# Steps moved by a slot in a hybrid decoder block's branches, and 96 instead of 128 stationary columns in one product of an inverse's doubling

## The chip, the cores and the metric

The kernel runs on one core of one Trainium2 chip. The metric is the device time of one execution in microseconds. The core has five engines with instruction queues of their own: PE (TensorE, matmuls, with weight loads shown apart as PEld), DVE (VectorE), ACT (ScalarE), POOL (GpSimd) and SP (SyncE, which here only issues DMAs). Each executes its instructions in order, and waits on semaphores for the others.

## The reference

One layer of a decoder on x of 256 x 2048, in float32. `h` is a normalised x; one input projection of h feeds three branches, whose outputs are gated, projected and summed; an MLP follows.

```python
h = rmsnorm(x, g_pre_mix)
proj = h @ w_in
aq, ak, av, az, ab, aa, bq, bf, bi, bz, cq, gates = split(proj)
qkv = silu(causal_dwconv(concat([aq, ak, av]), conv_a))
oa = gated_deltanet(aq, ak, av, sigmoid(ab), logdecay)   # 8 heads of 128, chunks of 64
oa = gated_head_norm(oa, az, gn_a)
ob = gated_head_norm(hgrn2(bq, bf, bi, lb), bz, gn_b)    # 8 heads of 128, chunks of 64
oc = memory_attention(cq, rmsnorm(mem, g_mem), w_kv_mem)
ga, gb, gc = split(sigmoid(gates))
merged = ga * (oa @ w_br_a) + gb * (ob @ w_br_b) + gc * (oc @ w_br_c)
x = x + rmsnorm(merged @ w_out, g_post_mix)
h2 = rmsnorm(x, g_pre_mlp)
x = x + rmsnorm(square(relu(h2 @ w_mlp_in)) @ w_mlp_out, g_post_mlp)
```

In `gated_deltanet` each chunk solves a unit lower triangular system of 64 x 64; in `hgrn2` the forget gate is `lb + (1 - lb) * sigmoid(f)`, taken in logarithms; `gated_head_norm` divides each head's output by its root mean square and multiplies by `silu(z)`.

## The kernel before

**Weights.** All large products are a stream of weight tiles of 256 rows by 512 columns (512 KB, 128 partitions by 2 x 512). SP's queue loads each into one of four buffers `w`. ACT casts it to float32r (`wh`), DVE forms the rest (`wl = w - wh`), and PE multiplies the two halves of the activations with them in three products: h with `wh`, h with `wl`, l with `wh` (`load_w`, `split_w`, `unit`). `wh` and `wl` have four buffers each as well. A tile of `unit` is 12 matmuls of 128 x 512; `unit_joined` forms a transposed result, with 16 matmuls of 512 and 256 columns per pair of halves. Counted from 0 in program order, tiles 192 to 199 belong to the forget projection of head group 1 (BF), 200 to 207 to its query (BQ), 208 to 223 to its BI and BZ, and 224 to 271 to branch 0: four turns j, each with eight tiles of the gate projection (G) and four of `w_br`. Branch 1 begins with tile 272 and its first `w_br` tile is 280; tiles from 320 on are `w_out`.

**Background steps.** Between the tiles, generators do the small work: `gen_a` (the delta rule of one head group), `gen_b` (the HGRN2 recurrence of one head group), `head_out` (the head norm, the transposes `oT` on PE, and their split into `oh` and `ol`), `gen_merge`, and the steps of `conv`, `z_evac` and `forget`, which go ahead of the others (`ahead_of_all`). `tick` runs after each tile and takes as many steps as a rate says, R1 to R4 by the part of the program. What a step issues stands at that place in the program; each `yield` ends a step. `pin` and `issue_after` keep an instruction at its place in its engine's queue; the other instructions of a step are put in order by the scheduler, by its own times and priorities. `drain` runs all steps that are left at once.

**Logarithms.** `exp_ln_table` issues an Abs on ACT and then the load of ACT's table for exponential and logarithm; Exp and Ln follow. It is used by `forget` (buffer `fe`) and by `gen_b` (buffer `bd`). Sigmoid and SiLU use another table.

**The inverse.** `gen_a` forms the inverse of the triangular system by doubling. At s = 32 blocks of 32 become blocks of 64: a product `pw`, a copy to `W`, and a second product `pzt`, whose stationary side is W of 128 x 128 for each of 8 blocks (two matrices of 64 in each), whose moving side is half of the columns of XT, and whose result is copied under a mask into XT. It runs once for each head group.

**Branches.** `branch(gi, o, w_br)` takes the gate's unit, a sigmoid of its PSUM into `sg`, the unit of `o` with `w_br`, and adds the product to `mg`. `o` is filled by `head_out`. Before branch 0 a loop pumps until `oa[1]` is there; behind it `drain` finishes `gen_b`, so that `ob` is there for branch 1. `load_gbc` issues two DMAs of 512 KB on ACT's queue; they broadcast a gain row.

Of the kernel before, what the change touches and what calls it, by code (L numbers as in the profile page):

```python
# [17 lines left out]
P = 128  # L18
# [15 lines left out]
KG = 2  # L34
BL = 16
WB = 4
R1, R2, R3, R4 = 1.1, 1.2, 1.2, 1.2


@with_exitstack  # L40
def tile_trunk(ctx: ExitStack, tc, a):
# [47 lines left out]
    def g4(name, shape=(P, 1024), dt=F32):  # L89
        return gp.tile(list(shape), dt, tag="g", name=nm(name))  # L90
# [11 lines left out]
    def bank(name):  # L102
        return pbp.tile([P, 512], F32, tag="bp", name=nm(name))
# [60 lines left out]
    def drain():  # L164
        while bg:
            pump(1)
# [608 lines left out]
    def head_out(o, z, rq, dst, hg):  # L775

        sq = g4("sq", (P, 8, P))
        A.activation(sq, o, AF.Square)
        ss = small("ss", 8)
        V.tensor_reduce(out=ss, in_=sq, axis=AX.X, op=ALU.add)  # L780
        yield
        if rq is not None:
            V.tensor_tensor(out=ss, in0=ss, in1=rq, op=ALU.mult)
            V.tensor_tensor(out=ss, in0=ss, in1=rq, op=ALU.mult)
        sc = rstd_of(ss, 8, P)
        if rq is not None:
            sc2 = small("sc2", 8)
            V.tensor_tensor(out=sc2, in0=sc, in1=rq, op=ALU.mult)
            sc = sc2
        on = g4("on", (P, 8, P))  # L790
        for b in range(8):
            V.scalar_tensor_tensor(out=on[:, b, :], in0=o[:, b, :], scalar=sc[:, b:b + 1], in1=z[:, b, :],
                                   op0=ALU.mult, op1=ALU.mult)
            if b % 4 == 3:
                yield
        hi, lo = g4("oh", (P, 4, S), F32R), g4("ol", (P, 4, S), F32R)
        for hh in range(2):
            pt = bank("oT")
            for q in range(2):
                for t in range(NT):  # L800
                    T.transpose(pt[:, q * S + t * P:q * S + (t + 1) * P], on[:, t * 4 + hh * 2 + q, :], ident)
            split_psum(pt.rearrange("p (q s) -> p q s", q=2), hi[:, hh * 2:hh * 2 + 2, :], lo[:, hh * 2:hh * 2 + 2, :])
        yield
        dst[hg] = (hi, lo)

    def gen_a(hg, kc, qc, vc, z):
# [167 lines left out]
        for s in (s_ for s_ in (2, 4, 8, 16, 32, 64) if s_ >= 2 * BL):  # L974
            last = s == 64
            pw = bank("pw")
            if last:

                for b in range(8):
                    T.matmul(pw[64:128, b * 64:(b + 1) * 64], U[0:64, b, 64:128], X[0:64, b, 0:64], start=True, stop=True)  # L980
                A.copy(W[64:128, :, 0:64], pw[64:128, :].rearrange("p (b s) -> p b s", b=8))
                yield
                pzt = bank("pzt")
                for b in range(8):
                    T.matmul(pzt[0:64, b * 64:(b + 1) * 64], W[64:128, b, 0:64], XT[64:128, b, 64:128],
                             start=True, stop=True)
                A.copy(XT[0:64, :, 64:128], pzt[0:64, :].rearrange("p (b s) -> p b s", b=8))
                yield
                break
            for b in range(8):  # L990
                T.matmul(pw[:, b * 64:(b + 1) * 64], U[:, b, :], half_view(X, s, False)[:, b], start=True, stop=True)
            A.copy(half_view(W, s, False), pw.rearrange("p (b n s) -> p b n s", b=8, s=s))
            yield
            pzt = bank("pzt")
            for b in range(8):
                T.matmul(pzt[:, b * 64:(b + 1) * 64], W[:, b, :], half_view(XT, s, True)[:, b],
                         start=True, stop=True)
            V.copy_predicated(half_view(XT, s, True), half_mask(mT[s], s, True),
                              pzt.rearrange("p (b n s) -> p b n s", b=8, s=s))
            yield  # L1000
            if s == 32:

                pt = bank("X")
                for b in range(8):
                    T.transpose(pt[0:64, b * 64:(b + 1) * 64], XT[0:64, b, 0:64], ident[0:64, 0:64])
                A.copy(X[0:64, :, 0:64], pt[0:64, :].rearrange("p (b i) -> p b i", b=8))
                yield
                continue
            for t in range(NT):
                pt = bank("X")  # L1010
                for h in range(4):
                    T.transpose(pt[:, h * P:(h + 1) * P], XT[:, t * 4 + h, :], ident)
                A.copy(X[:, t * 4:t * 4 + 4, :], pt.rearrange("p (h i) -> p h i", h=4))
            yield
# [67 lines left out]
    def branch(gi, o, w_br):  # L1082
        oact = act_of(o)
        for j in range(4):
            ps = unit(hact, KT, w_in, OFF_G + gi * D + 512 * j)
            sg = g4("sg", (P, NT, 512))
            own_table(A.activation(sg, ps.rearrange("p (t n) -> p t n", t=NT), AF.Sigmoid))
            ps = unit(oact, 8, w_br, 512 * j).rearrange("p (t n) -> p t n", t=NT)
            if gi == 2:
                mg[j] = g4("mg", (P, NT, 512))  # L1090
                V.tensor_tensor(out=mg[j], in0=ps, in1=sg, op=ALU.mult)
            else:
                V.tensor_tensor(out=sg, in0=ps, in1=sg, op=ALU.mult)
                V.tensor_tensor(out=mg[j], in0=mg[j], in1=sg, op=ALU.add)
            if gi == 1:
                bg.append(gen_merge(j))
# [4 lines left out]
    def forget(ps, hg):  # L1101

        t, g = g4("ft", (P, 4, S)), g4("fg", (P, 4, S))

        def steps():
            e = g4("fe", (P, 4, S))
            exp_ln_table(e, ps)
            pin(A.activation(e, e, AF.Exp, scale=-1.0))
            pin(A.activation(e, e, AF.Ln, bias=1.0))
            yield  # L1110
            yield
            V.scalar_tensor_tensor(out=t, in0=ps, scalar=0.0, in1=e, op0=ALU.max, op1=ALU.add)
            yield
            for h in range(4):
                c = hg * 4 + h
                A.activation(t[:, h, :], t[:, h, :], AF.Exp, scale=-1.0, bias=lbl1[:, c:c + 1])
            V.scalar_tensor_tensor(out=g, in0=ps, scalar=0.0, in1=e, op0=ALU.min, op1=ALU.subtract)
            yield

        ahead_of_all(steps())  # L1120
        return t, g

    def gen_b(hg, k, g, q, v, z):
# [9 lines left out]
                yield  # L1133
        exp_ln_table(d, d)
        pin(A.activation(d, d, AF.Exp, scale=-1.0))
        pin(A.activation(d, d, AF.Ln, bias=1.0))
        kq, kqh, kql = g4("kq"), g4("kqdh", dt=F32R), g4("kqdl", dt=F32R)
        V.tensor_tensor(out=kq, in0=k.rearrange("p h s -> p (h s)"), in1=q.rearrange("p h s -> p (h s)"), op=ALU.mult)
# [139 lines left out]
        bg.append(gen_b(hg, k, g, q, v, z))  # L1278
    rate[0] = R4

    while oa[1] is None:
        pump(1)
    branch(0, oa, a["w_br_a"][0])
    drain()


    def load_gbc(src):
# [4 lines left out]
            r.append(t)  # L1292
        return r

    gbc = load_gbc(a["g_post_mix"])
    branch(1, ob, a["w_br_b"][0])

    def gb(c):
        return gbc[c // 2][:, c % 2 * 512:c % 2 * 512 + 512]
# [210 lines left out]
```

## Time and profile before

| what | value |
|---|---|
| three runs | 1806.97, 1805.63, 1805.83 us; median 1805.83 |
| the profiled execution | 1805.44 us |
| its span, from first to last instruction | 1803.7 us |
| mean granted TensorE clock | 0.997 |
| ACT, DVE busy | 50%, 64% of the span |
| chain of work that ended last | PE 83% of the span, DVE 1%, ACT 1% |

The page lists for one execution the busy time of each engine, what ended the idle time of a group of instructions, and the chain followed back from the last instruction. In rows of the timeline the columns are start and duration in us, engine, line, operation, result and sources by their names, size and count, and in square brackets the idle time ahead with the engine and buffer that ended it. All rows have line 56, since a helper issues every instruction; so the names of the buffers tell them apart. `128*128` is the part of the array that a matmul uses. A matmul's row is longer than its share of the engine, since matmuls are pipelined: the distance from start to start counts.

### The profile page before, as it was taken

The numbers are of one execution on the slowest core, as the hardware profiler recorded it, in microseconds if no ns is written. First come the engines' busy times: TensorE is split into PE (matmuls) and PEld (weight loads), VectorE is DVE, ScalarE is ACT, GpSimd is POOL, SyncE is SP. The second block draws the span as 40 slices with busy tenths as digits, with TensorE's granted clock in tenths as the row PEclk, the third lists the DMA queues.
The fourth block names the chain that finished last, engine by engine and source line by source line (L and its number), as shares of the span: only waits on it lengthen the run. The fifth ranks groups of instructions, "written<-read, shape, count | busy, mean of one in ns | idle before, by whom it ended". The sixth has DMA issues, their size and how long they took to land.

```text
span 1803.7 us, 23759 instructions
## 1 busy us (share of the span) xinstructions
PE 1787.2 (99%) x9137; PEld 1522.9 (84%) x9137; DVE 1152.7 (64%) x1599; ACT 901.8 (50%) x1148; POOL 59.7 (3%) x100
## 2 busy tenths in 40 slices
PE   9999999999999999999999999999999999999998
PEld 7888888888888888888788888888888888888886
DVE  6865768684867577696555557555655565655556
ACT  6645566454554464555444445544444444444433
POOL 0000000400120000000000000000000000000000
PEclk9999999999999999999999999999999999999999
DMA  8665545875487455555666674666666666656563
GB/s 268 204 192 166 175 148 165 240 204 151 154 214 216 122 154 175 149 187 174 189 186 186 215 235 149 191 193 192 193 187 197 192 216 187 197 184 197 187 196 136
DMA packets 176226, 336.60 MB, mean 187 GB/s; under 512 B 13656, under 2 KB 15472, under 8 KB 175728
## 3 DMA queue, kind: packets, MB, share of 16 engines
q1 hardware_dynamic: 169280, 325.10, 58.7%
q0 software_dynamic: 2304, 5.44, 1.6%
q10 hardware_dynamic: 4528, 4.54, 0.9%
q8 instruction: 71, 1.16, 0.3%
q14 instruction: 43, 0.35, 0.1%
HBM read 332.75 MB, written 2.29 MB: 186 GB/s over the span
## 4 chain that ended last, share of the span: by engine, by line
PE 83%; DVE 1%; ACT 1%; issue 0%; POOL 0%; DVEq 0%; POOLq 0%
PE mm L56 78%; PE pa L56 1%; PE kk L56 0%; PE pzt L56 0%; PE pw L56 0%; PE bo L56 0%; PE o L56 0%; DVE on L56 0%; DVE wl L56 0%; POOL r L329 0%; PE tr L56 0%; ACT L56 0%; PE y L56 0%; PE mgT L56 0%; ACT bd L56 0%
## 5 line engine op out<-in xcount | busy, mean ns | idle before, releaser
L56 DVE TENSOR_TENSOR wl<-w,wh 128x1024 fp32r<-128x1024 f32 (+1 forms) x610 | 738.3, 1219 | 523.3 <-ACT wh L56 446.9
L56 ACT CAST wh<-w 128x1024 fp32r<-128x1024 f32 (+1 forms) x610 | 636.3, 1050 | 728.3 <-PE mm L56 632.0
L56 PE MATMUL mm<-wh,hh 128*128 128x512 f32 x1152 | 366.2, 392 | 0.0
L56 PEld LDWEIGHTS mm<-wh,hh 128*128 128x128 f32 x1152 | 216.2, 188 | 44.4
L56 PE MATMUL mm<-wl,hh 128*128 128x512 f32 x576 | 224.6, 390 | 0.0
L56 PE MATMUL mm<-h2h,wh 128*128 128x512 f32 x960 | 224.4, 390 | 0.0
L56 PEld LDWEIGHTS mm<-h2h,wh 128*128 128x128 f32 x960 | 178.3, 188 | 35.8
L56 PE MATMUL mm<-wh,mh 128*128 128x512 f32 x512 | 199.2, 389 | 0.0
L56 PE MATMUL mm<-wl,mh 128*128 128x512 f32 x512 | 199.2, 389 | 0.0
L56 PE MATMUL mm<-wh,ml 128*128 128x512 f32 x512 | 199.2, 389 | 0.0
L56 PE MATMUL mm<-hh,wh 128*128 128x512 f32 x768 | 185.9, 393 | 0.8 <-ACT z L56 0.8
L56 PEld LDWEIGHTS mm<-hh,wh 128*128 128x128 f32 x768 | 141.9, 189 | 29.0 <-ACT z L56 1.0
L56 PEld LDWEIGHTS mm<-wl,hh 128*128 128x128 f32 x576 | 108.2, 188 | 21.3
L56 PEld LDWEIGHTS mm<-h2h,wl 128*128 128x128 f32 x960 | 119.3, 192 | 2.3
L56 PE MATMUL mm<-h2h,wl 128*128 128x256 f32 x960 | 120.3, 283 | 0.0
L56 PEld LDWEIGHTS mm<-wh,mh 128*128 128x128 f32 x512 | 96.1, 188 | 20.0
L56 PEld LDWEIGHTS mm<-wl,mh 128*128 128x128 f32 x512 | 96.1, 188 | 19.9
L56 PEld LDWEIGHTS mm<-wh,ml 128*128 128x128 f32 x512 | 96.1, 188 | 19.9
L56 PE MATMUL mm<-hh,wl 128*128 128x256 f32 x768 | 103.8, 287 | 2.7 <-DVE wl L56 2.7
L56 PEld LDWEIGHTS mm<-hh,wl 128*128 128x128 f32 x768 | 100.4, 194 | 6.5 <-DVE wl L56 2.9
L56 PE MATMUL mm<-wh,oh 128*128 128x512 f32 x128 | 50.2, 392 | 0.0
L56 PE MATMUL mm<-wh,mgh 128*128 128x512 f32 x128 | 50.0, 390 | 0.0
(336 smaller groups left out, 1775.4 us busy)
## 6 DMA issues: line engine op xcount, KB each, us to landing
w<-in_w_in SPq DMA_DIRECT2D x240, 512.0 KB, 4.1
w<-in_w_mlp_in SPq DMA_DIRECT2D x128, 512.0 KB, 3.9
w<-in_w_mlp_out SPq DMA_DIRECT2D x128, 512.0 KB, 4.1
w<-in_w_out SPq DMA_DIRECT2D x32, 512.0 KB, 4.4
w<-in_w_kv_mem SPq DMA_DIRECT2D x30, 512.0 KB, 5.3
w<-in_w_br_c SPq DMA_DIRECT2D x16, 512.0 KB, 3.8
w<-in_w_br_a SPq DMA_DIRECT2D x16, 512.0 KB, 4.5
w<-in_w_br_b SPq DMA_DIRECT2D x16, 512.0 KB, 4.0
```

Source lines behind the costliest of these rows:

```text
L56: ins = op(*args, **kwargs)
```

## The change

Six edits of order and one of size:

- R4, the rate of steps from branch 0 on, is 1.25 instead of 1.2.
- `head_out` has one more `yield`, between the scaling `on` and the transposes `oT`.
- The second product of the doubling at s = 32 uses 96 of the 128 columns of W, and its result and the masked copy have 96 partitions. The lower 32 rows of a 128-row block hold nothing that the mask lets through.
- `branch` has the loop that pumps until `o[1]` is there between the gate's unit and the unit of `w_br`. The loop before branch 0 and the `drain` behind it are gone.
- `forget` begins with an empty step, and has a step's end between Exp and Ln, and one empty step less behind.
- `gen_b` has a step's end between Exp and Ln of `bd`.
- The two DMAs of `gbc` for the mixer are issued behind branch 1 instead of ahead of it.

```diff
-R1, R2, R3, R4 = 1.1, 1.2, 1.2, 1.2
+R1, R2, R3, R4 = 1.1, 1.2, 1.2, 1.25
...
             if b % 4 == 3:
                 yield
+        yield
         hi, lo = g4("oh", (P, 4, S), F32R), g4("ol", (P, 4, S), F32R)
...
-            pzt = bank("pzt")
+
+            pzt, m = bank("pzt"), P - s
             for b in range(8):
-                T.matmul(pzt[:, b * 64:(b + 1) * 64], W[:, b, :], half_view(XT, s, True)[:, b],
+                T.matmul(pzt[0:m, b * 64:(b + 1) * 64], W[:, b, 0:m], half_view(XT, s, True)[:, b],
                          start=True, stop=True)
-            V.copy_predicated(half_view(XT, s, True), half_mask(mT[s], s, True),
-                              pzt.rearrange("p (b n s) -> p b n s", b=8, s=s))
+            V.copy_predicated(half_view(XT[0:m], s, True), half_mask(mT[s], s, True)[0:m],
+                              pzt[0:m].rearrange("p (b n s) -> p b n s", b=8, s=s))
             yield
...
             own_table(A.activation(sg, ps.rearrange("p (t n) -> p t n", t=NT), AF.Sigmoid))
+            while o[1] is None:
+                pump(1)
             ps = unit(oact, 8, w_br, 512 * j).rearrange("p (t n) -> p t n", t=NT)
...
         def steps():
+            yield
             e = g4("fe", (P, 4, S))
             exp_ln_table(e, ps)
             pin(A.activation(e, e, AF.Exp, scale=-1.0))
+            yield
             pin(A.activation(e, e, AF.Ln, bias=1.0))
-            yield
             yield
             V.scalar_tensor_tensor(out=t, in0=ps, scalar=0.0, in1=e, op0=ALU.max, op1=ALU.add)
...
         exp_ln_table(d, d)
         pin(A.activation(d, d, AF.Exp, scale=-1.0))
+        yield
         pin(A.activation(d, d, AF.Ln, bias=1.0))
...
-    while oa[1] is None:
-        pump(1)
     branch(0, oa, a["w_br_a"][0])
-    drain()
...
+    branch(1, ob, a["w_br_b"][0])
     gbc = load_gbc(a["g_post_mix"])
-    branch(1, ob, a["w_br_b"][0])
```

How the rows move is shown at three places. The numbers behind a name tell buffers of one name apart; each program has numbers of its own.

The first place is ACT's queue in the query projection of head group 1, where the gate `fe` of that group and the chain `bd` of gen_b(0) are taken. `wh_6042` is tile 202 of the program before:

```order
L56 CAST oh_5896<-oT_5898 128x512
L56 CAST oh_5896<-oT_5905 128x512
L56 COPY sum_5724<-mm_5725 128x512
L56 ACTIVATE bd_5941<-bd_5941 128x1024
L56 ACT_TABLE_LOAD
L56 ACTIVATE bd_5941<-bd_5941 128x1024
L56 COPY sum_5724<-mm_5755 128x512
L56 ACTIVATE bd_5941<-bd_5941 128x1024
L56 ACTIVATE fe_6018<-sum_5724 128x1024
L56 ACT_TABLE_LOAD
L56 ACTIVATE fe_6018<-fe_6018 128x1024
L56 CAST wh_6042<-w_6040 128x1024
```

In the changed program the same place reads so; `wh_6023`, `wh_6029`, `wh_6069` and `wh_6075` are tiles 202 to 205:

```order
L56 CAST wh_6023<-w_6021 128x1024
L56 CAST wh_6029<-w_6027 128x1024
L56 COPY sum_5700<-mm_5731 128x512
L56 CAST oh_5950<-oT_5952 128x512
L56 CAST oh_5950<-oT_5959 128x512
L56 ACTIVATE fe_6013<-sum_5700 128x1024
L56 ACT_TABLE_LOAD
L56 ACTIVATE fe_6013<-fe_6013 128x1024
L56 CAST wh_6069<-w_6067 128x1024
L56 ACTIVATE fe_6013<-fe_6013 128x1024
L56 CAST wh_6075<-w_6073 128x1024
```

The chain `bd` is no longer here (it begins behind tiles 206 and 207), and casts of weights stand ahead of `fe` and between its Exp and Ln.

The second place is DVE's queue at the head norm of gen_b(0), in branch 0, where `on` is what PE transposes. Before, with `wl_6977` tile 239:

```order
L56 TENSOR_REDUCE ss_6862<-sq_6860 128x8
L56 TENSOR_TENSOR sg_6777<-mm_6779,sg_6777 128x1024
L56 TENSOR_SCALAR v_6882<-ss_6862 128x8
L56 TENSOR_TENSOR wl_6977<-w_6974,wh_6976 128x1024
L56 SCALAR_TENSOR_TENSOR on_6886<-ob_6843,r_6884,z_5722 128x128 x4
L56 TENSOR_TENSOR mg_3790<-mg_3790,sg_6777 128x1024
L56 SCALAR_TENSOR_TENSOR on_6886<-ob_6843,r_6884,z_5722 128x128 x4
L56 TENSOR_TENSOR wl_7007<-w_7004,wh_7006 128x1024
```

And in the changed program, with `wl_6942` tile 239 and `wl_7025` tile 242:

```order
L56 TENSOR_TENSOR sg_6756<-mm_6758,sg_6756 128x1024
L56 TENSOR_TENSOR wl_6942<-w_6939,wh_6941 128x1024
L56 TENSOR_TENSOR mg_3790<-mg_3790,sg_6756 128x1024
L56 TENSOR_TENSOR wl_6969<-w_6966,wh_6968 128x1024
L56 TENSOR_TENSOR wl_6991<-w_6988,wh_6990 128x1024
L56 TENSOR_REDUCE ss_6937<-sq_6935 128x8
L56 TENSOR_SCALAR v_6957<-ss_6937 128x8
L56 SCALAR_TENSOR_TENSOR on_6961<-ob_6900,r_6959,z_5698 128x128 x8
L56 TENSOR_TENSOR wl_7025<-w_7022,wh_7024 128x1024
```

The merge (`sg`, `mg`) and three residuals now stand ahead of the head norm, whose rows follow each other. On PE the transposes of this head group stand behind the last matmul of tile 241 instead of tile 237, those of head group 1 behind tile 277 instead of in two parts round tiles 272 and 273.

The third place is ACT's queue in branch 0's second turn. Before, with `wh_7142` tile 246 and `wh_7172` tile 247:

```order
L56 CAST wh_7142<-w_7140 128x1024
L56 ACT_TABLE_LOAD
L56 ACTIVATE sg_7095<-mm_6893 128x1024
L56 ACT_TABLE_LOAD
L56 ACTIVATE qp_7092<-bm_6968 128x8x64
L56 CAST wh_7172<-w_7170 128x1024
```

And in the changed program, with `wh_7120` tile 246 and `wh_7141` tile 247:

```order
L56 CAST wh_7120<-w_7118 128x1024
L56 ACT_TABLE_LOAD
L56 ACTIVATE sg_7068<-mm_6854 128x1024
L56 ACTIVATE bd_7041<-bd_7041 128x1024
L56 ACT_TABLE_LOAD
L56 ACTIVATE bd_7041<-bd_7041 128x1024
L56 CAST kqdh_7094<-kq_7093 128x1024
L56 ACTIVATE bd_7041<-bd_7041 128x1024
L56 CAST wh_7141<-w_7139 128x1024
L56 CAST wh_7170<-w_7168 128x1024
```

The chain `bd` of gen_b(1) and the cast `kqdh`, which stood about four tiles earlier, are now in this gap between two casts of weights; `qp` has gone behind them.

## The prediction

> **What bounds the kernel now.** I read the page's first part, then PE's waits in the region that the diff touches, then the windows and timelines round each wait. Weight tiles are numbered from 0 in program order; that order is the same in both programs.
>
> ```profile
> PE 1787.2 (99%) x9137; PEld 1522.9 (84%) x9137; DVE 1152.7 (64%) x1599; ACT 901.8 (50%) x1148; POOL 59.7 (3%) x100
> ```
>
> PE is busy for 99% of the span. An edit can pay only by removing PE work, a PE wait, or time at a lowered clock. PE's waits between 600 and 900 us:
>
> ```profile
> PE mm L56 <- DVE wl L56: 2.7, 1, 2.7
> PE oT L56 <- DVE on L56: 2.1, 4, 1.1
> ```
>
> The first wait stands in PE's timeline, and the windows give the clock behind it (columns: stretch, length, busy time of PE, PEld, DVE, ACT and POOL, then granted clock, DMA share, GB/s):
>
> ```profile
> 638.96 3.97 PE L56 MATMUL mm<-hh,wl 128*128 128x256 f32 x16 [2.67 <-DVE wl L56]
> 639.00:645.30 6.30, 6.30 (x23) 5.62 (x24) 5.73 (x6) 4.15 (x7) 0.00 (x0) 0.51 0.62 168
> 645.30:680.00 34.70, 34.70 (x174) 29.76 (x173) 31.02 (x48) 21.85 (x25) 0.00 (x0) 1.00 0.61 182
> ```
>
> PE stood for 2.67 us, and in the 6.30 us that follow TensorE had 0.51 of its clock, which costs (1 - 0.51) x 6.30 = 3.09 us more. After 645.3 the clock is 1.00. One late tile thus costs 5.76 us. ACT's timeline says why it was late:
>
> ```profile
> 622.13 1.05 ACT L56 CAST wh<-w 128x1024 fp32r<-128x1024 f32 x1 [0.76 <-PE mm L56]
> ...
> 628.53 1.06 ACT L56 ACTIVATE bd<-bd 128x1024 f32<-128x1024 f32 x1 [0.28 <-DVE bd L56]
> ...
> 633.29 1.05 ACT L56 ACTIVATE fe<-sum 128x1024 f32<-128x1024 f32 x1
> 634.36 1.28 ACT L56 ACT_TABLE_LOAD   x1
> 635.65 1.06 ACT L56 ACTIVATE fe<-fe 128x1024 f32<-128x1024 f32 x1
> 636.62 1.03 ACT L56 CAST wh<-w 128x1024 fp32r<-128x1024 f32 x1
> ```
>
> And DVE's row behind it:
>
> ```profile
> 637.68 1.23 DVE L56 TENSOR_TENSOR wl<-w,wh 128x1024 fp32r<-128x1024 f32 x1 [4.51 <-ACT wh L56]
> ```
>
> From 628.53 to 636.62 ACT works without a gap on two logarithm chains (`bd` of gen_b(0), then `fe` of hg 1) and one PSUM copy, 8.09 us in which no weight is cast. Tile 202's cast is behind them; DVE had waited 4.51 us for it.
>
> **Tile 202: -2.67 and -3.09.** In the new order ACT casts tiles 202 and 203 ahead of the `fe` chain, tiles 204 and 205 one on each side of its last `fe`, and the `bd` chain comes two casts later still (first fence of the change). The longest run without a cast there is one sum copy, two `oh` casts, `fe`, the table load and `fe`: about 0.5 + 1.1 + 1.07 + 1.29 + 0.97 = 4.9 us by the starts above. Walking these rows against PE's pace, tile 204 is ready some 5.5 us before its first matmul. So the wait goes, and with it the stretch at half clock.
>
> By the Trainium skill ("TensorE: Matmul & The Clock Gate", the table of Part 1) the clock falls after at least one idle window of about 3.4 us. This trace shows 0.51 right behind 2.67 us, so here the measurement decides. By the page's figure alone the 3.09 would have another cause and would stay.
>
> **The oT waits: -1.14 and -0.98.** head_out transposes `on` on PE too early. Two rows of its waits:
>
> ```profile
> 755.35 1.12 PE L56 MATMUL oT<-ident,on 128*128 128x128 f32 x7 [1.14 <-DVE on L56]
> 869.04 0.55 PE L56 MATMUL oT<-ident,on 128*128 128x128 f32 x3 [0.35 <-DVE on L56]
> ```
> ```profile
> 740.00:760.00 20.00, 18.86 (x102) 15.79 (x101) 13.25 (x21) 9.37 (x12) 2.54 (x1) 1.00 0.46 135
> ```
>
> The first is hg 0's; the other three of the 2.1 us, 0.98 together, are hg 1's, in 863 to 869. The chain that `oT` needs, in ACT's and DVE's timelines:
>
> ```profile
> 745.96 0.59 ACT L56 COPY ob<-bo 128x512 f32<-128x512 f32 x1 [1.14 <-PE bo L56]
> 746.58 1.06 ACT L56 ACTIVATE sq<-ob 128x1024 f32<-128x1024 f32 x1
> ```
> ```profile
> 747.67 1.22 DVE L56 TENSOR_REDUCE ss<-sq 128x8 f32<-128x1024 f32 x1 [2.09 <-ACT sq L56]
> ...
> 749.94 0.16 DVE L56 TENSOR_SCALAR v<-ss 128x8 f32<-128x8 f32 x1
> ...
> 752.76 1.14 DVE L56 SCALAR_TENSOR_TENSOR on<-ob,r,z 128x128 f32<-128x128 f32 x4 [1.53 <-POOL r L329]
> ...
> 754.95 1.13 DVE L56 SCALAR_TENSOR_TENSOR on<-ob,r,z 128x128 f32<-128x128 f32 x4
> ```
>
> From the end of `bo` (745.9) the chain takes 10.2 us, because DVE does `sg` ahead of `v`, and `mg` between the two halves of `on`. In the new order these, and the residual that stood there, are out of it (second fence of the change). What is left is 747.67 - 745.96 + 1.22 = 2.93, `v` 0.16, POOL's power (749.94 + 0.16 to 752.76) 2.66, and twice 1.13 of `on`: 8.0 us. `oT` comes four weight tiles after `bo` instead of three. A tile is 12 slots, and a slot is (775.00 - 773.64) / 6 = 0.227 by the rows quoted further down, so that four are 10.9 us and the margin is 2.9 us. hg 1 has the same pattern. Both waits go; the 1.14 us one did not lower the clock (the window round it, below), so nothing more comes with it. For oa[1] the step is later in the same way, and no wait stood there.
>
> **The doubling's second product: -0.7.** Two groups of 8 matmuls (16 records), one per head group. The group of 128 columns, and the nearest rows of 64, with the matmuls round them:
>
> ```profile
> 424.12 1.89 PE L56 MATMUL pzt<-XT,W 128*128 128x64 f32 x16
> ...
> 426.14 0.39 PE L56 MATMUL mm<-wl,hh 128*128 128x512 f32 x1
> ```
> ```profile
> 431.95 0.39 PE L56 MATMUL mm<-wh,hh 128*128 128x512 f32 x1
> 432.27 1.14 PE L56 MATMUL pw<-X,U 64*64 64x64 f32 x16
> 433.34 0.50 PE L56 MATMUL mm<-wh,hh 128*128 128x512 f32 x1
> 433.68 0.39 PE L56 MATMUL mm<-wl,hh 128*128 128x512 f32 x1
> ```
>
> The 128-column group costs 426.14 - 424.12 less one slot, 1.79 us. The 64-column one costs 433.68 - 431.95 less two slots, 1.28 us, in which a matmul ahead of it holds 0.32 and one behind it 0.34 instead of 0.227: 0.21 us for going in and out, 1.07 for itself. No row has 96 columns. Halfway between 1.07 and 1.79 is 1.43, a saving of 0.36 each, 0.7 for the two, if PE goes through them without the 0.21 (the built matmul keeps the full 128x128 tile). Ends: -1.0 for both if they cost what 64 do; +0.4 if nothing is saved and the 0.21 comes on top.
>
> By the Trainium skill ("TensorEngine Tiling (Array Packing)", Tiling Modes) column tiles are 128, 64 or 32 wide, and changing the mode drains TensorE. The rows at 432 fit that. If 96 columns were run in another mode, two drains would take 0.4 of the 0.7 back.
>
> **A new wait at tile 247: +0.5.** In branch 0's second turn ACT now has between the casts of tiles 246 and 247: table load, `sg`, the `bd` chain of gen_b(1) and `kqdh` (third fence of the change). Before, these stood in different tiles. The durations, from PE, ACT and DVE:
>
> ```profile
> 773.64 0.39 PE L56 MATMUL mm<-wh,oh 128*128 128x512 f32 x1
> ...
> 775.00 0.39 PE L56 MATMUL mm<-wh,oh 128*128 128x512 f32 x1
> ```
> ```profile
> 764.03 1.28 ACT L56 ACT_TABLE_LOAD   x1
> 765.32 1.06 ACT L56 ACTIVATE bd<-bd 128x1024 f32<-128x1024 f32 x1
> 766.29 1.03 ACT L56 CAST kqdh<-kq 128x1024 fp32r<-128x1024 f32 x1
> 767.22 1.06 ACT L56 ACTIVATE bd<-bd 128x1024 f32<-128x1024 f32 x1
> ...
> 773.84 1.03 ACT L56 ACTIVATE sg<-mm 128x1024 f32<-128x1024 f32 x1 [0.31 <-PE mm L56]
> ```
> ```profile
> 767.35 1.23 DVE L56 TENSOR_TENSOR kqdl<-kq,kqdh 128x1024 fp32r<-128x1024 f32 x1 [0.79 <-ACT kqdh L56]
> ...
> 769.63 1.22 DVE L56 TENSOR_TENSOR wl<-w,wh 128x1024 fp32r<-128x1024 f32 x1
> ```
>
> Count from the first matmul of tile 244, which follows the sigmoid's unit (773.64). `sg` starts at 0.20, the first `bd` at 1.15, the table load at 2.23, `bd` at 3.52, `kqdh` at 4.49, `bd` at 5.42, the cast of tile 247 at 6.38. DVE does `kqdl` at 4.49 + 1.06 = 5.55, `bm` one pitch (1.14) later, and tile 247's residual at 7.83, done at 9.05. PE is through three tiles at 36 x 0.227 = 8.17 and has two matmuls with `wh` to do, so it wants the residual at 8.62. With about 0.05 for the signal it waits 0.48 us. Queued behind on ACT is tile 248's cast, at 7.32, which PE needs 2.7 us later than tile 247's: no second wait. Bounds: nothing, if `sg` is earlier by that much; 1.6 us, if `kqdh` has to wait for one more operation of DVE (1.14) on its input's way.
>
> **Small ones.** In gen_a(1) the X transposes now stand four matmuls (0.91 us) behind `pzt`, whose predicated copy takes 0.7 us and starts some 0.2 us after: +0.1. The extra steps of forget, gen_b and head_out issue nothing. The raised rate moves steps by a part of a tile. The pump inside branch has nothing to run as a lump, since `oT` of hg 1 stands after tile 277 and branch 1's first product begins with tile 280; the removed pump and drain leave no lump either. ACT's two more table loads (1.28 us each) lie in ACT's free half. The two DMAs for `gbc` move from ACT's queue before branch 1 to between the casts of tiles 319 and 320:
>
> ```profile
> L119 ACTq DMA_DIRECT2D gbc<-in_g_post_mix x2: 342/396/450, 869.6 to 870.0; - x2
> ```
>
> They held ACT's queue 0.4 us each. Tile 320's buffer comes free three tiles, 8.2 us, before its first matmul; less the cast 1.05 and the residual 1.22 that leaves 5.9 us of cover, so they cost nothing; the tiles on SP's queue keep their order.
>
> **Sum**, against the profiled execution's 1805.44: - 2.67 - 3.09 - 1.14 - 0.98 - 0.7 + 0.5 + 0.1 = 1797.5. That execution is 0.39 under the median, so about **1797.8**. With the bounds of the product and of tile 247: 1796.5 to 1799.5.
>
> **Rivals.**
> - *The collision moves to tile 247.* The ACT block there is 6.2 us from `sg` to the cast, near the block of 8.09 that cost the clock. If `kqdh` or `sg` comes 2.2 us later than I walked it, PE waits 2.67 us and the clock halves: 2.2 + 3.09 more, 1803.1. For it: DVE's queue is full there, and `kqdh` waits on DVE's `kq`. Against it: 1.14 us of wait changed no clock. Chance 0.11.
> - *Tile 202 stays late,* because more than ACT's chains held it: 5.76 comes back, 1803.6. Against it: DVE's 4.51 us of waiting names ACT, and ACT has no gap before the cast. Moves that cancel out altogether belong here too. Chance 0.08.
> - *The half clock is not due to the wait:* 3.09 stays, 1800.9. Only its start right behind the gap ties them, but the windows before and behind are at 1.00. Chance 0.04.
> - *Slower: ACT's queue is held at the two DMAs for `gbc`.* Beyond 5.9 us of cover PE stands, one for one, plus 3.09 for the clock. It equals the time before from 10.8 us on (1797.8 - 5.9 + 3.09 + 10.8); two landings one after the other with tiles in between, say 18 us, give 1813. Against it: 0.4 us each in this trace, amid the same flow of weights. Chance 0.05.
>
> **How the numbers follow.** The forecast has 0.72. A change within 0.2% (3.6 us, so from 1802.2 to 1809.4) is about what a measurement of this kernel cannot tell from none. Faster: the forecast, the unchanged clock and a small part (0.02) of the moved collision, 0.78. Same: the rest of that and the late tile 202, 0.17. Slower: 0.05. The range takes in the forecast's own, with 1 us below for margins that I counted as used, and reaches up to the moved collision: 1795.5 to 1803.3, leaving out most of the late tile and the slower case.
>
> **What would show it.** No PE wait for `wl` near 639 us and no window at 0.51 there; no oT waits in 740 to 870; `pzt` records of 128x64 giving way to 96-column ones with a group near 1.4 us; a PE wait for `wl` of about half a microsecond in branch 0's second turn, at full clock; `gbc` issues still under half a microsecond. A second stretch at half clock anywhere behind 600 us would make the forecast wrong by 3 us or more.

## The result and the profile after

The changed kernel takes 1795.18 us, median of 6 runs (1794.28 to 1796.12), against 1805.73 us for the kernel before in runs beside it (6 runs, 1803.52 to 1807.40). The ratio is 0.9942, 95% interval 0.9929 to 0.9955: it is faster, by more than was forecast, and the time lies 0.3 us below the range. The profiled execution took 1796.12 us; that is the longest of the six, while the kernel before had been profiled near its median.

The page's first part for the changed kernel, and PE's waits between 600 and 900 us:

```profile
PE 1782.4 (99%) x9137; PEld 1520.4 (85%) x9137; DVE 1152.7 (64%) x1599; ACT 903.9 (50%) x1150; POOL 58.6 (3%) x100
```
```profile
PE mm L56 <- DVE wl L56: 0.2, 1, 0.2
```

Of 4.8 us of waits 0.2 are left. The windows of the same stretches (granted clock third from the end) have no half clock:

```profile
636.00:639.00 3.00, 3.00 (x20) 2.71 (x20) 3.00 (x4) 2.38 (x6) 0.00 (x0) 1.00 0.44 119
639.00:645.30 6.30, 6.30 (x32) 5.32 (x31) 5.74 (x11) 5.24 (x6) 0.00 (x0) 1.00 0.45 127
```

ACT's timeline there has tiles 202 and 203 in one row of two casts, then the `fe` chain with casts of weights between its steps; the `bd` chain comes later:

```profile
627.40 2.00 ACT L56 CAST wh<-w 128x1024 fp32r<-128x1024 f32 x2 [0.36 <-PE mm L56]
...
630.73 1.09 ACT L56 ACTIVATE fe<-sum 128x1024 f32<-128x1024 f32 x1
631.84 1.28 ACT L56 ACT_TABLE_LOAD   x1
633.13 1.07 ACT L56 ACTIVATE fe<-fe 128x1024 f32<-128x1024 f32 x1
634.10 1.03 ACT L56 CAST wh<-w 128x1024 fp32r<-128x1024 f32 x1
```

From 629.4, the end of tile 203's cast, to 634.10 no weight is cast: 4.7 us, and PE doesn't wait. In the kernel before it was 13.4 us, from 622.13 + 1.05 to 636.62, the last 8.1 of them without a gap on ACT. The head norm of hg 0, in ACT's, DVE's and PE's timelines:

```profile
747.66 0.59 ACT L56 COPY ob<-bo 128x512 f32<-128x512 f32 x1 [1.14 <-PE bo L56]
```
```profile
749.37 1.22 DVE L56 TENSOR_REDUCE ss<-sq 128x8 f32<-128x1024 f32 x1 [2.09 <-ACT sq L56]
750.63 0.17 DVE L56 TENSOR_SCALAR v<-ss 128x8 f32<-128x8 f32 x1
752.55 2.19 DVE L56 SCALAR_TENSOR_TENSOR on<-ob,r,z 128x128 f32<-128x128 f32 x8 [1.75 <-POOL r L329]
```
```profile
758.36 1.03 PE L56 MATMUL oT<-ident,on 128*128 128x128 f32 x8
```

`on` is done at 754.74, 7.1 us behind `bo`, and its transposes start 3.6 us later in one group without a wait.

### The profile page after: what moved, and what is told of

It is laid out like the page before. It is cut to its first block, busy times and chain, and to the rows that moved or that the text cites. A ratio compares the mean times of both kernels' runs of the same rounds, so it can differ in the third digit from the quotient of the medians.

```text
span 1794.4 us, 23765 instructions
## 1 busy us (share of the span) xinstructions
PE 1782.4 (99%) x9137; PEld 1520.4 (85%) x9137; DVE 1152.7 (64%) x1599; ACT 903.9 (50%) x1150; POOL 58.6 (3%) x100
## 3 DMA queue, kind: packets, MB, share of 16 engines
HBM read 332.75 MB, written 2.29 MB: 187 GB/s over the span
## 4 chain that ended last, share of the span: by engine, by line
PE 80%; issue 2%; DMA 1%; DVE 1%; POOL 1%; ACT 1%; DVEq 0%; POOLq 0%; ACTq 0%
PE mm L56 76%; PE pa L56 1%; DMA w<-in_w_in 1%; DMA scr<-U 0%; DMA lb<-scr 0%; PE pw L56 0%; PE o L56 0%; PE bo L56 0%; DVE wl L56 0%; PE pzt L56 0%; PE kk L56 0%; POOL scr L893 0%; PE tr L56 0%; PE y L56 0%; PE mgT L56 0%
## 5 line engine op out<-in xcount | busy, mean ns | idle before, releaser
L56 PE MATMUL mm<-wl,oh 128*128 128x512 f32 x128 | 49.9, 390 | 0.2 <-DVE wl L56 0.2
```

The lines of the kernel that those rows point to most:

```text
L56: ins = op(*args, **kwargs)
```

## The experiments

Times are compared with runs of the kernel before on the same chip: 1804.2 us (20 runs) for e1 to e4, 1804.0 (15) for e6 to e8, 1804.51 (9) for e10 and e11. A place's cost is told as the distance from matmul to matmul less the median distance of the same form, summed from the trace; this takes in waits, restarts (the extra time of the first matmuls behind a wait) and a lowered clock. From e6 to e11 a difference to e1 is one between chips, on which the kernel before differs by up to 0.3 us.

**e1, the changed kernel again.**

> The changed kernel once more, unchanged. Theory A (my sum was right in its places; it priced each wait at the idle time of its row, while the distance between matmuls shows 0.1 to 0.2 us more for each, and the profiled execution of the changed kernel was a late one): the ratio comes out at 0.994 again, about 10.5 us under before, and the profile, with no wait of PE for the sum near 527 us, has a span of about 1793.5. Rival B (that wait belongs to the changed order): it is there again at 0.7 us, and the profiled span is 1794.4 again.

Measured: 1794.74 us (5 runs, 1794.31 to 1795.22), ratio 0.9949 (0.9936 to 0.9961), span 1793.5. The first profile's wait near 527 us was

```profile
527.93 2.12 PE L56 MATMUL mm<-hh,wh 128*128 128x512 f32 x8 [0.73 <-DVE sum L56]
```

and here PE has none there. DVE was late in that execution behind the landing of a weight tile: ACT's cast had waited 5.81 us for it, against 4.31 in e1, and DVE 4.05 for the cast, against 2.40. Theory A holds in the wait and the span; by the medians the difference is 9.5 us and not 10.5. A wait of 0.7 us comes and goes between runs of one program.

**e2, the product alone.** The kernel before with

```diff
-                T.matmul(pzt[:, b * 64:(b + 1) * 64], W[:, b, :], half_view(XT, s, True)[:, b],
+                T.matmul(pzt[0:m, b * 64:(b + 1) * 64], W[:, b, 0:m], half_view(XT, s, True)[:, b],
...
```

> The kernel before with the 96 columns alone. Theory A: two groups at 1.38 instead of 1.79 us, so 0.8 us less than before (ratio 0.9995); the wait of 2.67 at tile 202, the window at half clock and the oT waits all stay. Rival C (the 2.6 us by which the forecast was too high sit in the product: what follows it moves too): 2 us less or more.

Measured: 1803.84 us (11 runs, 1801.98 to 1804.96), ratio 0.9996 (0.9987 to 1.0005): 0.4 us by the medians, which these runs cannot tell from nothing. The rows can tell, here in the changed kernel's PE timeline:

```profile
423.67 1.49 PE L56 MATMUL pzt<-XT,W 128*96 128x64 f32 x16
...
425.28 0.39 PE L56 MATMUL mm<-wl,hh 128*128 128x512 f32 x1
```

A group takes 425.28 - 423.67 - 0.227 = 1.38 us instead of 1.79, so 0.8 less for both; e2's own two groups have the same distances. That is a little below the 1.43 which I had taken, and without the cost of going in and out that the 64-column groups have. The times alone do not exclude rival C, since the interval reaches 2.3 us; against it stand the profile, in which the waits of 2.7 us at tile 202 and of 2.1 us for `on` are as before, and e3.

**e3, the moves alone.** The changed kernel with all 128 columns (e2's line undone).

> The changed kernel with 128 columns in the product again: every move of steps, without the smaller product. Theory A: 10.5 - 0.8 = 9.7 us under before (ratio 0.9946), no half clock, no oT wait. Rival C: 8 us under before or less.

Measured: 1795.41 us (5 runs, 1795.20 to 1796.75), ratio 0.9954 (0.9941 to 0.9966), 8.8 us under the kernel before on its chip and 0.67 over the changed kernel of e1. No window at half clock, no wait for `on`. Theory A's 9.7 was a little high, since e1's own difference was 9.5 and not 10.5; with the 0.8 of the product the parts add up.

**e4, forget alone.** The kernel before with

```diff
         def steps():
+            yield
             e = g4("fe", (P, 4, S))
             exp_ln_table(e, ps)
             pin(A.activation(e, e, AF.Exp, scale=-1.0))
+            yield
             pin(A.activation(e, e, AF.Ln, bias=1.0))
-            yield
             yield
```

> The kernel before with the moved steps of forget alone. The order of ACT has tile 202's cast ahead of the logarithm chains here too; the transposes of hg 0 stand four tiles behind bo, those of hg 1 two and a half. Theory A: 5.9 (wait with its restart 2.8 and half clock 3.05) and 1.3 for hg 0's transposes come off, the waits of hg 1 stay: 7.2 us under before (ratio 0.996). Rival D (the half clock has another cause than the wait): only 4.1 us come off, and a window at half clock stays near 640 us.

Measured: 1799.58 us (10 runs, 1799.18 to 1800.87), ratio 0.9976 (0.9967 to 0.9985): 4.6 us, not 7.2. The wait at tile 202 and its half clock are gone, and so is hg 0's wait for `on`, so these few lines would have done for both. But delays of 0.1 to 0.3 us, about 1 us together, are left between 625 and 655, and two other waits stand in PE's timeline:

```profile
773.09 0.50 PE L56 MATMUL mm<-wl,oh 128*128 128x512 f32 x1 [0.76 <-DVE wl L56]
862.07 0.30 PE L56 MATMUL oT<-ident,on 128*128 128x128 f32 x1 [1.78 <-DVE on L56]
```

The second is hg 1's, longer than before, because PE is ready for its transposes 3.7 us behind `bo` (`bo` ends at 856.64, and 862.07 - 1.78 is 860.29). The half clock went with the wait, against rival D.

**e5, idle work on ACT.** The changed kernel, and ahead of one cast in twelve units of the MLP's second product

```diff
...
+        j = g4("held", (P, 8, P))
+        for n in range(int(2 * hold[0]) // 2):
+            pin(A.copy(j, ident.unsqueeze(1).to_broadcast([P, 8, P])))
...
```

> The changed kernel with idle work on ACT ahead of one cast of a weight at twelve places of the MLP's second product, in two series of 9, 9.5, 10, 10.5, 11 and 12 copies of 0.96 us, so that PE stands for about 1, 1.5, 2, 2.5, 3 and 4 us, each length twice. It leaves nothing out. Theory A (the half clock is due to PE's standing, from some length between 1.14 and 2.67 us on): the places with 2.5 us and more show a stretch of about 6 us at half clock behind them, each of both series, those of 1 and 1.5 us show none; each wait costs 0.1 to 0.2 us more, from matmul to matmul, than the idle time of its row. Rival E (a fixed window that runs by itself decides): of two places with one length, between 1.5 and 3 us, one shows the half clock and the other doesn't. Rival D (another cause): no place shows it, or all do.

It took 1850.25 us. The waits came out alike in both series; the clock did not. PE's idle time at the first matmul, the distance to it beyond one slot, and the granted clock of the 6 us behind it (from the windows):

| copies | idle, us (1st, 2nd series) | distance beyond a slot, us | clock, 1st series | clock, 2nd series |
|---|---|---|---|---|
| 9 | 0.85, 0.84 | 1.01, 1.00 | 1.00 | 1.00 |
| 9.5 | 1.46, 1.46 | 1.62, 1.62 | 0.72 | 1.00 |
| 10 | 1.93, 1.92 | 2.09, 2.08 | 1.00 | 0.72 |
| 10.5 | 2.53, 2.53 | 2.69, 2.69 | 0.72 | 1.00 |
| 11 | 3.00, 3.00 | 3.16, 3.16 | 0.72 | 0.55 |
| 12 | 4.03, 4.03 | 4.20, 4.20 | 0.50 | 0.72 |

Two of these windows, for the same wait of 2.53 us:

```profile
1396.00:1402.00 6.00, 5.47 (x16) 4.13 (x17) 4.54 (x4) 3.38 (x4) 0.00 (x0) 0.72 0.60 190
1688.00:1694.00 6.00, 5.38 (x22) 4.16 (x23) 4.63 (x4) 3.72 (x5) 0.00 (x0) 1.00 0.59 192
```

Theory A's fixed length falls and rival E holds: of equal waits between 1.46 and 2.53 us one lowers the clock and the other does not; at 3.0 and 4.0 it fell each time, for longer or shorter. The wait costs 0.16 us more than its idle time at each place. In eleven of the twelve places a second wait of 0.5 to 0.8 us, for the residual, stands a few matmuls behind it.

What decides between equal waits is in the same trace. Its record of the clock changes only in steps of 3.41 us: the clock is half for 3.41 or 6.83 us, and full between for whole multiples of that (92.2 us is 27 steps, 68.3 is 20). So 0.72 over 6 us is 3.41 us at half clock. Cut at these steps, the stretches round the two waits of 2.53 us are

```profile
1393.74:1397.15 3.41, 0.73 (x2) 0.30 (x2) 1.24 (x2) 3.38 (x5) 0.00 (x0) 1.00 0.00 0
1397.15:1400.57 3.42, 3.38 (x8) 2.71 (x9) 3.39 (x3) 1.57 (x2) 0.00 (x0) 0.50 0.63 189
1400.57:1403.98 3.41, 3.41 (x16) 2.83 (x16) 1.56 (x2) 1.05 (x1) 0.00 (x0) 1.00 1.02 365
1683.87:1687.29 3.42, 1.69 (x8) 1.07 (x6) 0.00 (x0) 3.32 (x5) 0.00 (x0) 1.00 0.00 0
1687.29:1690.70 3.41, 2.08 (x8) 1.43 (x9) 2.63 (x3) 3.41 (x4) 0.00 (x0) 1.00 0.11 13
```

The first wait lies almost whole in one step, where PE is idle for 2.68 us, and the next step is at half clock. The second is divided, 1.73 us and 1.33 with the wait behind it, and the clock stays. Over all the traces, without their starts and ends, a step at full clock with 2.1 us of PE's idle time or more was followed by half clock each time (nine), one with 1.55 or less never; of five between 1.63 and 1.92, two were.

The Trainium skill ("TensorE: Matmul & The Clock Gate", What's actually happening) says that activity is judged in windows of about 3.4 us that run freely. The steps of 3.41 us agree with that. By the Trainium skill ("TensorE: Matmul & The Clock Gate", HAM oscillation — how this bites in real kernels) only gaps of PE over about 3.4 us are to be avoided. That is too lax here: a wait of 1.46 us was followed by half clock.

**e6, R4 = 1.3.**

```diff
-R1, R2, R3, R4 = 1.1, 1.2, 1.2, 1.25
+R1, R2, R3, R4 = 1.1, 1.2, 1.2, 1.3
```

> The changed kernel with R4 = 1.3. ACT's queue has tile 247's cast behind a longer block (three table loads), but the first Abs, table load and Exp of bd now stand ahead of sg, where ACT would else wait for the gate's unit. Transposes stay four tiles behind bo. Theory A: behind sg are a table load, Ln and kqdh, so the cast starts 4.5 us behind tile 244's first matmul instead of 6.4: no wait at 247, and 0.45 us less than the changed kernel. Rival B (the length of the block counts): a wait of 1.7 us or more there, with or without half clock, 1.3 to 5 us more than the changed kernel.

Measured: 1799.32 us (11 runs, 1798.70 to 1802.34), ratio 0.9978 (0.9969 to 0.9987), 4.6 us more than the changed kernel in e1. Theory A falls. PE's timeline:

```profile
772.14 0.74 PE L56 MATMUL ad<-kqdh,onesr 128*128 128x512 f32 x2 [0.81 <-ACT kqdh L56]
...
782.43 0.50 PE L56 MATMUL mm<-wl,hh 128*128 128x512 f32 x1 [1.55 <-DVE wl L56]
```

I had looked at the cast of tile 247 and not at the step behind: `ad` now comes so early that PE waits for `kqdh`. The time is what rival B had, 1.3 to 5 us more, though the wait is divided and its larger part stands further on. It is also the first rival of the prediction, the collision that moves. The profiled run had full clock behind the 1.55 us (1.00 in the window from 782 to 788). Whether the clock was halved in the longest runs, which took up to 1802.34 us, is not known, since only the shortest has a profile.

**e7, R4 = 1.3 and two empty steps in head_out.**

> The changed kernel with R4 = 1.3 and a second empty step ahead of the transposes of head_out. The chain bd of gen_b(1) is at tile 249, away from sg; transposes stand five tiles behind bo; in the input projections of hg 1 a block of 6.9 us stands ahead of tile 212's cast. Theory A: no wait at 247 to 249, and at most 0.3 us at 212, where ACT's cover is 5.9 us with a tile's lead: 0.2 to 0.5 us less than the changed kernel. Rival B (the collision moves again): a wait of 1 us or more at 212.

Measured: 1796.87 us (5 runs, 1796.07 to 1797.68), ratio 0.9959 (0.9945 to 0.9972), 2.1 us over e1. There is no wait at tile 212 and one of 0.32 us behind 780, so ACT's cover was right; but at another place, one that neither theory named, PE waits for DVE:

```profile
629.70 2.14 PE L56 MATMUL mm<-hh,wh 128*128 128x512 f32 x8 [1.32 <-DVE sum L56]
```
```profile
627.91 1.14 DVE L56 SCALAR_TENSOR_TENSOR on<-oa,sc,z 128x128 f32<-128x128 f32 x4
628.96 0.68 DVE L56 TENSOR_TENSOR sum<-mm,sum 128x512 f32<-128x512 f32 x1
```

The head norm of oa[1] stands ahead of the sum that frees the PSUM bank.

**e8, no added step in head_out.** The changed kernel without the second `yield` ahead of `hi, lo`.

> The changed kernel without the added step in head_out. The transposes stand three tiles behind bo again for both head groups; tile 247 has a block of 5.1 us in place of 7.4. Theory A (the distance from bo to the transposes decides): a wait for on at both head groups, 1 to 2 us each, none at 247: 1.5 to 3 us more than the changed kernel. Rival (the order on DVE, with sg and mg out of the chain, is what removed the waits): no wait for on, and 0.45 us less than the changed kernel.

Measured: 1796.83 us (4 runs, 1795.74 to 1798.01), ratio 0.9959 (0.9945 to 0.9972), 2.1 us over e1 by the medians and 1.4 by the spans. The rival holds for the transposes: three tiles behind `bo`, and no wait for `on`. Its rows on ACT and PE:

```profile
745.60 0.59 ACT L56 COPY ob<-bo 128x512 f32<-128x512 f32 x1 [1.14 <-PE bo L56]
```
```profile
753.58 1.03 PE L56 MATMUL oT<-ident,on 128*128 128x128 f32 x8
```

What removed hg 0's wait is that `sg` and `mg` are out of DVE's chain; the fourth tile was not needed for it. The wait at tile 247 is gone too, as the rival had it. The kernel is longer all the same, with two waits for `sum` in the input projections (0.32 and 0.42 us in the profile, 0.48 and 0.58 from matmul to matmul) and smaller delays round them.

**e9, e12 and e13, the kernel before three times more, and e14, the changed kernel a third time.**

> The kernel before, unchanged, for one more profile. Theory E (the clock is decided by a window that runs by itself, so that the same wait costs 0 to 3 us more): the wait of 2.67 us at tile 202 is there again, within 0.1 us, and the stretch at half clock behind it begins elsewhere and is shorter or longer than 6.30 us, or isn't there. Theory A as the prediction had it: 6.3 us at half clock right behind the wait again.

> The kernel before once more, to see what its runs differ in (they lie between 1802.7 and 1807.4 us). Theory E (the stretch at half clock behind tile 202's wait is what varies, 0 to 3 us): the time follows the price of that place, wait and clock together, between 2.8 and 5.8 us, and is 1803 where the stretch is short. Rival F (that place costs 5.2 to 5.8 us each time, since PE runs into the next late residual where the clock is whole): the place stays within 0.6 us, and the time differs elsewhere, at the start or around 530 us.

> As for the look before this one: by theory E the price of tile 202's place follows the time, by rival F it stays between 5.2 and 5.8 us.

> The changed kernel a third time. Theory E: no stretch at half clock, so its time lies within 0.8 us of 1795, with no wait behind 600 us but that of tile 247, 0.45 us from matmul to matmul. Rival F says the same of these places, and that what differs from the other two looks stands at the start and around 530 us, up to 0.9 us.

They took 1805.06, 1803.76, 1805.19 and 1795.41 us. In e12 the wait at tile 202 was followed by no half clock at all, but by a second wait, in which PE overtook the next residual. PE's timeline and the window:

```profile
639.28 1.22 PE L56 MATMUL mm<-hh,wl 128*128 128x256 f32 x8 [2.68 <-DVE wl L56]
641.17 1.21 PE L56 MATMUL mm<-hh,wl 128*128 128x256 f32 x8 [0.68 <-DVE wl L56]
```
```profile
641.00:644.00 3.00, 2.83 (x16) 2.53 (x17) 3.00 (x4) 2.47 (x5) 0.00 (x0) 1.00 0.89 270
```

In e9 the same two waits stood, and the clock of the 6.3 us behind was 0.73 instead of the 0.51 of the first profile. The steps of 3.41 us explain it: half clock lasted 6.83 us in the first profile (from 638.40), 3.41 in e9 (from 640.94) and in e13 (from 639.86). In e12 the step that ends at 638.40 had 1.80 us of the wait, where it had 2.11 in the first profile. Place by place, over all these profiles (us, from matmul to matmul):

| place | before: first, e9, e12, e13 | mean | changed: first, e1, e14 | mean | difference |
|---|---|---|---|---|---|
| start, 0 to 60 | 2.41, 1.82, 2.22, 2.43 | 2.22 | 2.27, 1.73, 2.29 | 2.10 | -0.12 |
| 60 to 500 | 4.20, 4.06, 4.17, 4.16 | 4.15 | 3.90, 4.33, 4.09 | 4.11 | -0.04 |
| 500 to 560 | 0.23, 0.99, 0.79, 1.24 | 0.81 | 1.11, 0.38, 0.34 | 0.61 | -0.20 |
| tile 202, 625 to 655 | 6.19, 5.77, 4.21, 4.73 | 5.22 | 0.07, 0.07, 0.06 | 0.07 | -5.16 |
| 740 to 800: oT of hg 0, tile 247 | 1.53, 1.50, 1.52, 1.53 | 1.52 | 0.62, 0.58, 0.61 | 0.60 | -0.92 |
| 800 to 880: oT of hg 1 | 2.29, 2.30, 2.33, 2.35 | 2.32 | 0.39, 0.39, 0.39 | 0.39 | -1.93 |
| the product | 2 x 1.79 | 3.58 | 2 x 1.38 | 2.76 | -0.82 |

The four places that the change touches give 8.8 us; the mean times of these executions, 1804.86 and 1795.58, differ by 9.3. Theory E is right about the wait, which came back within 0.02 us, and about the clock, which varied; but neither E nor F accounts for the times alone. Tile 202's place varies by 2 us from run to run, and the cheapest profile is the one without half clock (e12, also the shortest of the four), but e13 has a cheap one and a long time, with its surplus at 500 to 560.

**e10, R4 = 1.3 and one more step in gen_b.**

```diff
         pin(A.activation(d, d, AF.Exp, scale=-1.0))
         yield
+        yield
         pin(A.activation(d, d, AF.Ln, bias=1.0))
```

> The changed kernel with R4 = 1.3 and one more empty step between Exp and Ln of bd in gen_b. At tile 247 the block on ACT is sg and the first half of bd, 1.9 us shorter than in the changed kernel, without kqdh and Ln. The transposes stay four tiles behind bo. If the wait there is ACT's block, as I worked it out, it goes: no PE wait behind 600 us, 0.3 to 0.5 us less than the changed kernel. If, as with R4 = 1.3 alone, steps behind the block are late in their turn: a wait for wl or kqdh of 0.5 us or more, and no gain.

Measured: 1795.94 us (5 runs, 1795.82 to 1796.20), ratio 0.9951 (0.9938 to 0.9963), 1.2 us over e1, though the intervals of the two ratios overlap almost whole. No wait is left at tile 247 itself, but a little further on one of 0.87 us stands; PE's row, and DVE's queue ahead of it:

```profile
779.92 0.50 PE L56 MATMUL mm<-wl,hh 128*128 128x512 f32 x1 [0.87 <-DVE wl L56]
```
```profile
775.18 1.23 DVE L56 TENSOR_TENSOR sg<-mm,sg 128x1024 f32<-128x1024 f32 x1 [0.93 <-PE mm L56]
776.32 1.28 DVE L56 TENSOR_TENSOR AT<-ad,ident 128x512 f32<-128x512 f32 x2
777.52 1.22 DVE L56 TENSOR_TENSOR mg<-mg,sg 128x1024 f32<-128x1024 f32 x1
778.65 1.22 DVE L56 TENSOR_TENSOR wl<-w,wh 128x1024 fp32r<-128x1024 f32 x1
```

The residual stands behind the merge and `AT`: with ACT relieved, DVE is the late one.

**e11, R4 = 1.45.**

> The changed kernel with R4 = 1.45. The logarithm chain of gen_b(1) stands at tile 245, in a block of 5.1 us, sg one tile on, in 4.1 us; transposes four tiles behind bo. If cover of 5.9 us holds for both: no PE wait behind 600 us, 0.3 to 0.5 us less than the changed kernel. If the two blocks add up: a wait at tile 246 or 247 of about 5.1 + 4.1 + 1.0 - 5.9 - 2.7 = 1.6 us, with or without half clock, 1 to 5 us more than the changed kernel.

Measured: 1796.88 us (5 runs, 1796.25 to 1797.61), ratio 0.9956 (0.9943 to 0.9970), 2.1 us over e1. A wait stands there again, of half of the 1.6 us that I had worked out for two blocks that add up; whether they do is not shown:

```profile
771.43 0.50 PE L56 MATMUL mm<-wl,oh 128*128 128x512 f32 x1 [0.76 <-DVE wl L56]
```

None of e6, e7, e10 and e11 beats the changed kernel; no version better than it was found. R4, the step in gen_b, the pump in `branch` and the move of `gbc` were not run alone, so the 4 us that e4 and e2 leave are not divided among them.

## Why the prediction was too cautious

**Direction and places: right.** The places came out as forecast: no late tile 202, no half clock, no waits for `on`, a loss of half a microsecond at tile 247, `gbc` issued in 0.34 to 0.46 us each without harm:

```profile
L119 ACTq DMA_DIRECT2D gbc<-in_g_post_mix x2: 342/398/455, 978.7 to 979.1; - x2
```

None of the rivals occurred in the changed kernel; the moved collision came in e6.

**The oT waits: the term that was mis-sized.** This is the step that failed. I had written -1.14 and -0.98, which are the idle times in the rows' brackets; the waits cost 1.30 and 1.93 us. The row ahead of the first wait in the kernel before was

```profile
753.94 0.27 PE L56 MATMUL oT<-ident,on 128*128 128x128 f32 x1
```

so that from matmul to matmul this wait cost 755.35 - 753.94 - 0.11 = 1.30, with 0.11 for the transpose's own slot. For hg 1 three waits cut the transposes in pieces. The first two, in PE's timeline of the kernel before, are

```profile
862.75 0.30 PE L56 MATMUL oT<-ident,on 128*128 128x128 f32 x1
863.28 0.30 PE L56 MATMUL oT<-ident,on 128*128 128x128 f32 x1 [0.23 <-DVE on L56]
863.98 0.59 PE L56 MATMUL oT<-ident,on 128*128 128x128 f32 x3 [0.40 <-DVE on L56]
```

Each piece has a restart of its own, 0.16 to 0.19 us at the wait and up to 0.11 at the matmuls round it; the place gave 1.93. The difference, 0.16 + 0.95 = 1.1 us, is the largest part of what the sum lacked. e5 shows the same surplus, 0.16, at the first matmul of all twelve waits.

**From the sum to a time.** The table's first columns redo the sum on the execution that it started from. Tile 202's place gives 6.19 - 0.07, the transposes and tile 247 give 1.53 - 0.62 and 2.29 - 0.39, the product 0.82: 9.75 us, so 1795.7 where the sum had 1797.5. Of these 1.8 us, 1.1 are the oT waits, 0.36 are tile 202, and 0.1 each are the product and the X transposes; the rest is spread. What is left between 1797.8 and 1795.18 is the 0.39 added for the median, and 0.5, which is within the changed kernel's own runs (1794.28 to 1796.12).

With 1.1 us more for the oT waits the forecast would have been 1796.7 and the range would have begun at 1794.4, which holds the measured time. The bounds were also added up wrongly: from 1797.8, a product of -1.0 to +0.4 and a wait of 0 to 1.6 at tile 247 give 1797.0 to 1800.0, not 1796.5 to 1799.5. And 1 us below them was little, since runs of one kernel lie 2 to 4 us apart.

Part of the result's 10.6 us is chance or the chip: e1 gave 9.5, and the profiles 9.3. On three chips of the experiments the kernel before had medians of 1804.0 to 1804.5 us, on a fourth runs of 1803.76, 1805.19 and 1806.17. Whether the chip or chance makes that difference was not separated.

**Tile 202: right in its cause, a draw in its size.** -2.67 and -3.09 gave 5.76; the place cost 6.12 more than in the changed kernel in that execution, and 5.16 in the mean over four. The cause, two logarithm chains behind one another on ACT ahead of a cast, is shown by e4, where the steps of `forget` alone part the two chains. That the half clock belongs to the wait is shown by e5, but not with a fixed price: it lasts 0, 3.41 or 6.83 us by how the wait lies to the steps of the clock. Where it doesn't come, the next residual is late (0.68 in e12), which gives part of it back.

**The product: right.** 0.41 per group against 0.36, and no switch. I had kept the 0.21 as a bound because no row had 96 columns. I had also written that the matmul keeps the full 128x128 tile; the profile names it `128*96`. Still the matmul behind the group holds 0.31 us, as behind the 128-column group (0.32), and the one ahead 0.23, a plain slot. By the Trainium skill ("TensorEngine Tiling (Array Packing)", Tiling Modes) a change of mode drains. The rows of `128*96` show no such cost.

**Tile 247: right in size, and half right in cause.** 0.45 us from matmul to matmul against 0.48, though the row's idle time is only 0.18. PE's row, and ACT's and DVE's ahead of it:

```profile
773.76 0.50 PE L56 MATMUL mm<-wl,oh 128*128 128x512 f32 x1 [0.18 <-DVE wl L56]
```
```profile
769.14 1.04 ACT L56 CAST kqdh<-kq 128x1024 fp32r<-128x1024 f32 x1
770.08 1.05 ACT L56 ACTIVATE bd<-bd 128x1024 f32<-128x1024 f32 x1
771.03 1.99 ACT L56 CAST wh<-w 128x1024 fp32r<-128x1024 f32 x2
```
```profile
771.35 1.22 DVE L56 TENSOR_TENSOR bm<-bm,bd 128x1024 f32<-128x1024 f32 x1
772.49 2.35 DVE L56 TENSOR_TENSOR wl<-w,wh 128x1024 fp32r<-128x1024 f32 x2
```

The cast starts 6.34 us behind tile 244's first matmul (764.69), where I had 6.38, and DVE's `bm` holds the residual until 772.49, 7.80 where I had 7.83. But e10 shows that relieving ACT there doesn't pay, since the merge and `AT` hold the residuals of the next tiles.

**The X transposes: wrong, by 0.1.** No wait came behind the product's copy; the place from 560 to 625 costs 1.2 us in both kernels.

## What to carry to other kernels

Price a wait that is to go by the distance from one instruction to the next, not by the idle time in its row, and count the pieces that it cuts a group into. Where a wait also lowers the clock, price it over several profiles: one execution is one draw. In a stream of tiles that two helper engines prepare, look at the longest run of other work ahead of each tile on both of them; moving a chain from one gap is worth it only if the gaps where it lands have room, on the second engine too, as e6, e7, e10 and e11 show.

## What the runs showed of the hardware that was not expected

- The granted clock changed only in steps of 3.41 us, and half clock lasted one or two of them. What counted was PE's idle time within one step: after 2.11 us and more the clock was halved in nine of nine, after 1.55 and less never, after 1.63 to 1.92 in two of five (before, e2, e4, e5, e6, e9, e12, e13).
- So equal waits of PE, of 1.46, 1.93 and 2.53 us, lowered the clock to 0.72 over the next 6 us at one place and left it at 1.00 at the other (e5). The same wait of 2.67 to 2.69 us in one program was followed by 0.51, by 0.73 and by 1.00 (first profile, e9, e12).
- A fp32 group of 16 records with 96 stationary columns takes 1.38 us against 1.79 with 128, 0.77 of it where the columns are 0.75, and enters and leaves without the 0.2 us that groups on a 64x64 tile cost.
- Resuming after a wait cost 0.16 us beyond the idle time on the first matmul of 512 columns, whatever the wait's length between 0.85 and 4 us (twelve of twelve in e5); at tile 247 of the changed kernel it was 0.27.
